# The second MLP matrix as seven half-block products for eight, aligned operand rings, and recurrent stages one behind the other

## The chip, the cores and the metric

The kernel runs on one core of a Trainium2 chip. Times are device microseconds of that core. Times that differ by less than about 0.2% cannot be told apart for this kernel (its three runs span 0.05%).

## The reference

The kernel computes two post-norm layers on a sequence of 1024 tokens of width 1024, in float32. Layer 0 mixes with sliding-window attention beside a gated DeltaNet, layer 1 with a Griffin recurrent block; each is followed by an MLP of hidden width 4096 with squared ReLU. What the change touches is this:

```
def rg_lru(x, w_a, b_a, w_x, b_x, lam):
    r = sigmoid(einsum('bthi,hij->bthj', xh, w_a) + b_a)
    i = sigmoid(einsum('bthi,hij->bthj', xh, w_x) + b_x)
    a = exp(-LRU_C * r * softplus(-lam))
    b = sqrt(-expm1(2 * log a)) * (i * x)
    h_t = a_t * h_{t-1} + b_t            (associative scan over time)

def recurrent_mixer(x, ...):
    xr, gate = split_cols(x @ w_in, (LRU_WIDTH, LRU_WIDTH))
    xr = causal_dwconv(xr, conv_w, conv_b)
    return (rg_lru(xr, ...) * gelu(gate)) @ w_out

def sqrelu_mlp(x, w1, w2):
    h = relu(x @ w1)
    return (h * h) @ w2

each layer:  x <- LN(alpha*x + mixer(x));  x <- LN(alpha*x + sqrelu_mlp(x))
```

## The kernel before

The 1024 tokens are worked as two chunks of 512, called stream 0 and stream 1. Each stream is a Python generator that runs hybrid mixer, output projection, layer norm, MLP of layer 0, layer norm, recurrent mixer (four `rec_block`s), output projection, layer norm, MLP of layer 1, layer norm. The only carry between streams is small (convolution halos, last recurrent state, attention keys).

**Precision.** Every large product is made of three float32r products: a value is split into a rounded high part and a low part, and `mm3` issues high x high, high x low and low x high into one PSUM bank. The split is a copy (mostly ScalarE, every fifth on VectorE) and a subtraction (alternately VectorE and GpSimd; `HV`, `LG`). Weights are split as they arrive (`wblock`: a 512 KB load into a `ws` tile, then tiles `wh` and `wl`); activations are split once.

**MLP.** `mlp` works through eight blocks `e` of 512 hidden units. For each of four slices `f` of 128 hidden units, `proj_fm` makes 24 matmuls of 128x512 (w1 stationary, all 512 tokens moving), then relu, square and split give two `s` tiles. Then w2 is applied: for each half of the output (512 columns), four PSUM banks (one for each 128 tokens) collect 4 slices x 3 matmuls with the `s` tile stationary and the weight moving, and VectorE adds each bank to the running output `y`, which lies in `g` tiles. That is 96 + 96 matmuls in a block and 8 additions from PSUM. The last block of the whole program has its weights split ahead and finishes token tile by token tile.

**Recurrent block.** One `rec_block` makes four projections of 24 matmuls (two with convolution, two for the gelu gate) and 24 gate matmuls, 120 in all, with tanh, exp, sqrt, a scan and products on ScalarE, VectorE and GpSimd in between.

**Order of the work.** All matmuls are put in one order by `Clock`, a rough model of the engines that asks at each step which generator's next product has its operands; small mixers (attention, DeltaNet, layer norm) come in between when their operands are due. The streams are taken by `phase` (0 goes first, and MLP 0 is phase 1, MLP 1 phase 2), so a recurrent block goes ahead of an MLP of the other stream and MLP matmuls fill its waits. Before the change, stream 0 waits behind its layer-0 MLP until stream 1 has its first layer norm (`ln1`), so the recurrent blocks of stream 0 lie beside stream 1's MLP of layer 0; stream 1 waits for `rec`, so its recurrent blocks lie beside stream 0's MLP of layer 1. The other engines take their work in the order in which it was written down; SyncE's queue issues the weight loads, ScalarE's a few others.

**Buffers.** `g`: 14 tiles of 2048 floats a partition; `t`, `s`, `f`: rings of 11, 9 and 4 tiles of 516 floats. A tile of 516 floats takes 2080 bytes, so every second tile of these rings starts 32 bytes off a multiple of 64; the tiles `g`, `ws`, `wh` and `wl` all start at multiples of 64.

## Time and profile before

| what | value |
|---|---|
| median of 3 runs | 2387.83 us (2387.71 to 2388.8) |
| span of the profiled execution | 2384.5 us, so 3.3 us of the median lie around it |
| granted TensorE clock, mean | 0.992 |
| TensorE busy | 2298.9 us (96%) |
| VectorE, ScalarE, GpSimd busy | 56%, 38%, 35% |
| DMA | 227.43 MB, mean 95 GB/s |

PE is TensorE's matmuls, PEld its weight loads (they overlap), DVE is VectorE, ACT ScalarE, POOL GpSimd. Nearly every instruction stands under one line, that of the helper which records it (L177 for the three elementwise engines, L204 for matmuls), so groups are read by tile names, `out<-in`. A matmul's row lasts about 0.39 us because matmuls are pipelined; what a matmul costs is the distance from one start to the next.

### The profile page before, as it was taken

The numbers are of one execution on the slowest core, as the hardware profiler recorded it, in microseconds if no ns is written. First come the engines' busy times: TensorE is split into PE (matmuls) and PEld (weight loads), VectorE is DVE, ScalarE is ACT, GpSimd is POOL, SyncE is SP. The second block draws the span as 40 slices with busy tenths as digits, with TensorE's granted clock in tenths as the row PEclk, the third lists the DMA queues.
The fourth block names the chain that finished last, engine by engine and source line by source line (L and its number), as shares of the span: only waits on it lengthen the run. The fifth ranks groups of instructions, "written<-read, shape, count | busy, mean of one in ns | idle before, by whom it ended". The sixth has DMA issues, their size and how long they took to land. (4 is left out here: it accounts for less than half of the span.)

```text
span 2384.5 us, 33354 instructions
## 1 busy us (share of the span) xinstructions
PE 2298.9 (96%) x12724; PEld 1841.9 (77%) x12724; DVE 1345.1 (56%) x2550; ACT 912.7 (38%) x1813; POOL 843.0 (35%) x706
## 2 busy tenths in 40 slices
PE   8889997999999999999999999999999999999997
PEld 7666775677777878778887788877887788778876
DVE  7697659565754463755664623565665543633345
ACT  5364424443333242454443322344554232322331
POOL 3342334232332243433443432343333333433341
PEclk9999998999999999999999999999999999999999
DMA  4121231122233222322333222232325222332231
GB/s 154 54 81 31 81 124 36 54 69 74 73 114 110 95 88 98 123 89 97 98 131 125 82 96 97 97 121 91 98 93 177 85 97 97 107 115 98 98 117 51
DMA packets 67487, 227.43 MB, mean 95 GB/s; under 512 B 7424, under 2 KB 7808, under 8 KB 67328
## 3 DMA queue, kind: packets, MB, share of 16 engines
q1 hardware_dynamic: 58832, 204.01, 25.9%
q10 hardware_dynamic: 8496, 21.30, 2.5%
q8 instruction: 100, 1.64, 0.3%
q14 instruction: 59, 0.48, 0.1%
HBM read 216.89 MB, written 8.39 MB: 94 GB/s over the span
## 5 line engine op out<-in xcount | busy, mean ns | idle before, releaser
L177 POOL TENSOR_TENSOR wl<-ws,wh 128x512 fp32r<-128x512 f32 (+1 forms) x372 | 497.6, 1338 | 1261.4 <-ACT wh L177 979.4
L204 PE MATMUL mm<-g,wh 128*128 128x512 f32 x2816 | 886.7, 396 | 0.5 <-DVE g L177 0.5
L177 ACT CAST wh<-ws 128x512 fp32r<-128x512 f32 (+1 forms) x595 | 365.5, 616 | 993.0 <-PE mm L204 910.1
L204 PE MATMUL mm<-wh,s 128*128 128x512 f32 x1984 | 648.2, 399 | 11.4 <-ACT s L177 5.7
L204 PEld LDWEIGHTS mm<-g,wh 128*128 128x128 f32 x2816 | 520.2, 189 | 107.2 <-issue 2.9
L204 PE MATMUL mm<-g,wl 128*128 128x512 f32 x1408 | 550.9, 391 | 5.4 <-POOL wl L177 5.4
L204 PEld LDWEIGHTS mm<-wh,s 128*128 128x128 f32 x1984 | 374.0, 189 | 102.6 <-ACT s L177 6.2
L204 PE MATMUL mm<-wl,s 128*128 128x512 f32 x992 | 391.9, 395 | 2.3 <-POOL wl L177 1.4
L177 DVE TENSOR_TENSOR wl<-ws,wh 128x512 fp32r<-128x512 f32 (+1 forms) x372 | 281.2, 756 | 188.8 <-ACT wh L177 184.4
L204 PEld LDWEIGHTS mm<-g,wl 128*128 128x128 f32 x1408 | 265.1, 188 | 64.0 <-POOL wl L177 7.1
L204 PE MATMUL mm<-wh,g 128*128 128x512 f32 (+1 forms) x768 | 235.2, 380 | 10.0 <-ACT wh L177 6.1
L177 DVE TENSOR_TENSOR s<-s,s 128x512 fp32r<-128x512 f32 x128 | 100.4, 784 | 242.9 <-POOL s L177 231.1
L204 PEld LDWEIGHTS mm<-wl,s 128*128 128x128 f32 x992 | 187.4, 189 | 43.3 <-POOL wl L177 1.8
L177 DVE TENSOR_TENSOR g<-g,mm 128x512 f32<-128x512 f32 x224 | 144.0, 680 | 130.7 <-PE mm L204 130.5
L204 PEld LDWEIGHTS mm<-wh,g 128*128 128x128 f32 x768 | 142.0, 190 | 38.7 <-ACT wh L177 6.1
L177 DVE CAST wh<-ws 128x512 fp32r<-128x512 f32 (+1 forms) x149 | 73.8, 495 | 172.6 <-PE mm L204 165.0
L177 POOL TENSOR_TENSOR s<-s 128x512 f32<-128x512 f32 x128 | 145.3, 1135 | 26.4 <-ACT s L177 26.4
L204 PE MATMUL mm<-wl,g 128*128 128x512 f32 (+1 forms) x384 | 143.7, 374 | 0.1
L177 ACT ACTIVATE s<-mm 128x512 f32<-128x512 f32 x128 | 75.9, 593 | 62.1 <-PE mm L204 61.9
L177 ACT ACTIVATE s<-s 128x512 fp32r<-128x512 f32 (+1 forms) x136 | 83.5, 614 | 19.0 <-DVE s L177 8.0
L204 PEld LDWEIGHTS mm<-wl,g 128*128 128x128 f32 x384 | 72.9, 190 | 11.9 <-DVE wl L177 0.4
L204 PE MATMUL mx<-g,wh 128*128 128x512 f32 x256 | 78.8, 389 | 0.0
(209 smaller groups left out, 2230.3 us busy)
## 6 DMA issues: line engine op xcount, KB each, us to landing
ws<-w SPq DMA_DIRECT2D x256, 512.0 KB, 3.3
ws<-hin_fm SPq DMA_DIRECT2D x32, 512.0 KB, 3.3
ws<-rin SPq DMA_DIRECT2D x32, 512.0 KB, 3.3
ws<-hout SPq DMA_DIRECT2D x16, 512.0 KB, 3.4
ws<-rout SPq DMA_DIRECT2D x16, 512.0 KB, 3.4
t<-ln ACTq DMA_DIRECT2D x28, 256.0 KB, 4.2
ws<-hin_q SPq DMA_DIRECT2D x8, 512.0 KB, 3.2
g<-x ACTq DMA_DIRECT2D x8, 512.0 KB, 5.0
```

The source lines that it names most:

```text
L177: r = f(*a, **k)
L204: return self._pe(self.pe.matmul(out, lhsT, rhs, start=start, stop=stop), out, [lhsT, rhs], c, start)
```

## The change

It has five parts.

1. **Seven products for eight** (`fast_w2`, `Fast`). A block's hidden activations (512 tokens x 512 hidden units) are seen as 2 x 2 blocks: two halves of 256 tokens, and the two slices of a pair `p`; w2 as two slices by two halves of the output. A Strassen form (with the sums of Winograd's variant) needs seven block products. Sums of activations (`s1` to `s4`) are formed in `hidden`, sums of weights (`t1` to `t4`) in `fast_w2`, in float32 before they are split. Four of the products are accumulated one on another in the same two PSUM banks (`X`), with the banks read between products; two others share a pair of banks (`R`). Every product's two banks are added to or subtracted from a quarter of `y`: 84 matmuls and 14 additions from PSUM. A block is worked so only where five `g` tiles are free when it begins (`begin`); the rest keep eight products. In the built program 23 of the 32 blocks are of the new kind, and the program has 10854 matmuls for 11130.
2. **The order within the MLP.** The first slice of block e+1 goes ahead of block e's w2 products.
3. **Rings and tiles.** `t` and `s` tiles are 512 floats, `f` tiles 528, so all start at multiples of 64 bytes; the `s` ring has 14 tiles. The DMA scratch area at the start of the memory is 1024 bytes for 16384. `wh` and `wl` are two tiles of 1024 floats for four of 512, so one copy and one subtraction split a whole load.
4. **w2 in another layout**: one load of 1 MB for a pair of slices, into a `g` tile (new blocks), or two strided 512 KB loads (old ones).
5. **Recurrent stages in a row.** Stream 0 waits until stream 1's layer-0 MLP has emitted its last w1 slice (`m7`), then the four blocks of both streams follow each other in turn (`rb`), stream 1's with `s` tiles for `t` tiles. The layer norm behind stream 1's output projection waits for `m7` of stream 0 (`hold`).

```diff
-WB, HV, LG = 4, 5, 2
-RINGS = dict(t=11, s=9, f=4)
+WB, WS, HV, LG = 2, 3, 5, 2
+RINGS = dict(t=11, s=14, f=4)
+FW = 528
...
     def tl(r, dt=F32):
-        return take(r, tpool.tile([P, 516], dt, tag=r, name=nm(r), bufs=RINGS[r]))
+        return take(r, tpool.tile([P, FW if r == "f" else 512], dt, tag=r, name=nm(r), bufs=RINGS[r]))
...
+    def split(h, l, x, key):
+        wcount[0] += 1
+        (V.tensor_copy if wcount[0] % HV == 0 else S.copy)(h, x)
+        (G if key else V).tensor_tensor(l, x, h, ALU.subtract)
...
+    def fast_w2(e, src, fast, hid, yg, ls):
...
+        for p in range(2):
+            DS.dma_start(fast.w[p], src[e * 2 + p])
+        X = [mm_ps() for _ in range(2)]
+        R = None
+        for i, (a, b, acc, out, sign, done) in enumerate((
+                ("a11", "b11", "X", (0, 0), 1, False), ("a12", "b21", "R", (0, 0), 1, True),
+                ("s2", "t2", "X", (0, 1), -1, False), ("s1", "t1", "R", (1, 1), 1, False),
+                ("s3", "t3", "X", (1, 1), -1, True), ("s4", "b22", "R", (0, 1), 1, True),
+                ("a22", "t4", "X", (1, 0), 1, True))):
+            if i in (1, 3):
+                R = [mm_ps() for _ in range(2)]
+            start = i in (0, 1, 3)
...
+                h, l = ts("t", F32R), ts("t", F32R)
+                split(h, l, x, (i + p) % 2)
+                if b == "b11":
+                    V.tensor_tensor(t1, b11, b12, ALU.add)
+                    V.tensor_tensor(t2, t1, b22, ALU.add)
+                    G.tensor_tensor(t3, b12, b22, ALU.add)
+                elif b == "b21":
+                    V.tensor_tensor(t4, t2, b21, ALU.add)
...
+            for p in range(2):
+                ah, al = hid[p][a]
+                for t in range(2):
+                    ps = (X if acc == "X" else R)[t]
+                    mm3(ps, ah[:, t * P:(t + 1) * P], al[:, t * P:(t + 1) * P], *hl[p], start and p == 0, p == 1, not start)
+                    if p == 1:
...
+                            V.tensor_tensor(y, y, ps, op)
...
+            S.activation(z, ps, AF.Relu)
+            S.activation(z, z, AF.Square)
+            if f % 2:
+                V.tensor_tensor(B[:, 0:512], A[:, 256:768], A[:, 512:1024], ALU.subtract)
+                V.tensor_tensor(B[:, 512:768], B[:, 256:512], A[:, 256:512], ALU.subtract)
+                V.tensor_tensor(B[:, 768:1024], A[:, 0:256], B[:, 512:768], ALU.add)
+                own = [ts("s", F32R) for _ in range(7)]
+                hl = [own[0:2], own[2:4], own[4:6], (own[6][:, 0:256], own[6][:, 256:512])]
+                for i, z in enumerate((A[:, 0:512], B[:, 512:1024], B[:, 0:512], A[:, 768:1024])):
+                    S.copy(hl[i][0], z)
+                    (G if i > 1 else V).tensor_tensor(hl[i][1], z, hl[i][0], ALU.subtract)
...
-        if c == 0:
-            yield from wait(lambda: "ln1" in st[1])
-        else:
-            yield from wait(lambda: "rec" in st[0])
         hT = ActT()
         light[c] = True
         for b in range(4):
+            yield from wait(lambda: c == 0 or sts[0].get("rb", 0) > b)
             if b % 2 == 0:
                 yield from need("g", 2)
-            yield from rec_block(c, b, s["x"], hT, s)
+            yield from rec_block(c, b, s["x"], hT, s, "ts"[c])
+            st[c]["rb"] = b + 1
```

**How the instructions move.** On TensorE, in the MLP of layer 1, before (`mm_` a PSUM bank, `wh`, `wl` the split weights that move, `s_` the stationary activations): the third slice of a half goes to four banks, which stay the block's banks over all four slices.

```order
L204 MATMUL mm_12845<-wh_12885,s_12796 128x512
L204 MATMUL mm_12845<-wl_12886,s_12796 128x512
L204 MATMUL mm_12845<-wh_12885,s_12797 128x512
L204 MATMUL mm_12846<-wh_12885,s_12796 128x512
L204 MATMUL mm_12846<-wl_12886,s_12796 128x512
L204 MATMUL mm_12846<-wh_12885,s_12797 128x512
L204 MATMUL mm_12847<-wh_12885,s_12796 128x512
L204 MATMUL mm_12847<-wl_12886,s_12796 128x512
```

After, in a block of the new kind (`t_` holds the split weight sums): the end of product `s4 x b22` in the `R` banks, and the start of `a22 x t4` in the `X` banks, which then hold their fourth product.

```order
L205 MATMUL mm_17694<-t_17744,s_17568 128x512
L205 MATMUL mm_17694<-t_17745,s_17568 128x512
L205 MATMUL mm_17694<-t_17744,s_17569 128x512
L205 MATMUL mm_17695<-t_17744,s_17568 128x512
L205 MATMUL mm_17695<-t_17745,s_17568 128x512
L205 MATMUL mm_17695<-t_17744,s_17569 128x512
L205 MATMUL mm_17616<-t_17762,s_17488 128x512
L205 MATMUL mm_17616<-t_17763,s_17488 128x512
L205 MATMUL mm_17616<-t_17762,s_17488 128x512
L205 MATMUL mm_17617<-t_17762,s_17488 128x512
```

Two token tiles share a product where there were four, and a bank is read and gone on with, not given back.

On VectorE, in the w2 part of a block in the MLP of layer 1, before: additions of banks to `y` (`g<-g,mm`) in fours, with weight splits between.

```order
L177 TENSOR_TENSOR g_16126<-g_16126,mm_19271 128x512
L177 TENSOR_TENSOR wl_19388<-ws_19385,wh_19387 128x512
L177 TENSOR_TENSOR g_16126<-g_16126,mm_19272 128x512
L177 TENSOR_TENSOR g_16127<-g_16127,mm_19273 128x512
L177 TENSOR_TENSOR g_16127<-g_16127,mm_19274 128x512
L177 CAST wh_19389<-ws_19385 128x512
L177 TENSOR_TENSOR wl_19426<-ws_19423,wh_19425 128x512
L177 TENSOR_TENSOR g_16126<-g_16126,mm_19347 128x512
```

After:

```order
L178 TENSOR_TENSOR g_14144<-g_14144,mm_17616 128x512
L178 TENSOR_TENSOR g_14144<-g_14144,mm_17617 128x512
L178 TENSOR_TENSOR s_17569<-g_17276,s_17568 128x512
L178 TENSOR_TENSOR t_17701<-g_17273,t_17700 128x512
L178 TENSOR_TENSOR g_14144<-g_14144,mm_17646 128x512
L178 TENSOR_TENSOR t_17719<-g_17272,t_17718 128x512
L178 TENSOR_TENSOR g_14144<-g_14144,mm_17647 128x512
L178 CAST t_17722<-g_17273 128x512
L178 TENSOR_TENSOR g_14144<-g_14144,mm_17616 128x512
L178 TENSOR_TENSOR g_14144<-g_14144,mm_17617 128x512
L178 TENSOR_TENSOR t_17745<-g_17273,t_17744 128x512
L178 TENSOR_TENSOR g_14145<-g_14145,mm_17694 128x512
```

Additions now come two for every product of 12 matmuls, with the splits of the next products queued between them, and bank 17616 is read four times in a block.

On ScalarE, in the recurrent stage, before (`f<-mm` the projection's copy, `s<-mm` the relu of the other stream's MLP):

```order
L177 ACTIVATE s_15021<-mm_14994 128x512
L177 ACTIVATE s_15019<-s_15021 128x512
L177 CAST g_14447<-t_14748 128x512
L177 CAST wh_15124<-ws_15122 128x512
L177 CAST g_14447<-t_14830 128x512
L177 COPY f_15026<-mm_15041 128x512
L177 ACTIVATE t_15028<-f_15026,sm 128x512
L177 ACTIVATE f_15027<-f_15026,sm 128x512
```

After:

```order
L178 COPY f_12540<-mm_12551 128x512
L178 CAST t_12452<-t_12451 128x512
L178 CAST g_12440<-s_12273 128x512
L178 ACTIVATE f_12541<-f_12540,sm 128x512
L178 ACTIVATE t_12542<-f_12540,sm 128x512
L178 CAST s_12498<-s_12497 128x512
L178 CAST wh_12670<-ws_12668 128x1024
L178 COPY f_12586<-mm_12597 128x512
```

No MLP work stands between any more: stream 0's block (`t` tiles) alternates with stream 1's (`s` tiles). From the first to the last matmul of the recurrent blocks the new order has 1264 matmuls: the blocks' own 960, 192 of stream 0's output projection, 64 transposes of layer norms and 48 of an MLP. Before, that stretch had 3568, of which 2352 were MLP.

## The prediction

> **What bounds the kernel now.** I read the page first, then the chain of waits, then stretches of time, then the groups of instructions by form, and last single rows. From the page, the span, the busy times, and TensorE's busy tenths in 40 slices:

> ```profile
> span 2384.5 us, 33354 instructions
> PE 2298.9 (96%) x12724; PEld 1841.9 (77%) x12724; DVE 1345.1 (56%) x2550; ACT 912.7 (38%) x1813; POOL 843.0 (35%) x706
> PE   8889997999999999999999999999999999999997
> ```

> TensorE works nearly throughout; only the first eight slices (the hybrid mixers) and the last show gaps. The chain of waits in order of time (start, length, engine and line, links) has long stretches of nothing else:

> ```profile
> 2089.11 223.08 PE mm L204 x971
> ```

> 223.08 us over 971 matmuls is 230 ns each: there matmul follows matmul, and taking matmuls out shortens the chain. Four stretches (busy us and counts of PE, PEld, DVE, ACT, POOL, then granted clock, DMA share, GB/s): MLP alone; the recurrent blocks of stream 0 beside stream 1's MLP; the stretch with the worst gap; the first fifth.

> ```profile
> 2100.00:2280.00 180.00, 180.00 (x786) 147.30 (x785) 56.83 (x94) 51.35 (x85) 58.68 (x49) 1.00 0.29 94
> 1000.00:1260.00 260.00, 257.90 (x1127) 211.01 (x1126) 146.30 (x188) 126.11 (x204) 96.48 (x89) 1.00 0.31 104
> 360.00:420.00 60.00, 44.91 (x394) 33.24 (x394) 55.85 (x135) 29.85 (x72) 28.05 (x21) 0.86 0.10 33
> 0.00:480.00 480.00, 433.53 (x3625) 329.13 (x3626) 353.79 (x892) 210.34 (x575) 170.09 (x160) 0.98 0.23 76
> ```

> In the MLP TensorE never stops and VectorE is busy 32% of the time. Where VectorE is at 74% (0 to 480) TensorE loses 10%, where it is at 93% (360 to 420) TensorE loses 25%. That is the measure for what follows: the change takes work from TensorE and gives work to VectorE and GpSimd.

> **Fewer matmuls.** The w2 matmuls by form (w2 is `wh,s` and `wl,s`):

> ```profile
> L204 PE MATMUL mm<-wh,s 128*128 128x512 f32 x1984 | 648.2, 399 | 11.4 <-ACT s L177 5.7 <-ACT f L177 4.2 <-DVE g L177 1.4
> L204 PE MATMUL mm<-wl,s 128*128 128x512 f32 x992 | 391.9, 395 | 2.3 <-POOL wl L177 1.4 <-DVE wl L177 0.9
> ```

> 1984 + 992 = 31 blocks of 96, with hardly a wait. The means near 400 ns are latencies; the price is the distance of starts. From the timeline, every third matmul of a w1 slice (`g,wl`) and of w2 (`wl,s`):

> ```profile
> 1940.05 0.39 PE L204 MATMUL mm<-g,wl 128*128 128x512 f32 x1
> ...
> 1947.53 0.39 PE L204 MATMUL mm<-g,wl 128*128 128x512 f32 x1
> ...
> 1948.67 0.39 PE L204 MATMUL mm<-wl,s 128*128 128x512 f32 x1
> ...
> 1969.56 0.40 PE L204 MATMUL mm<-wl,s 128*128 128x512 f32 x1
> ```

> w1: 11 triples in 7.48 us, 226.7 ns a matmul. w2: 30 triples in 20.89 us, 232.1 ns. The change removes 12 matmuls in each of 23 blocks, 276 in all: 276 x 232.1 = **-64.1 us**.

> **Aligned operands.** The two kinds of matmul differ in where their operands lie: `g`, `wh`, `wl` start at multiples of 64 bytes, `s` tiles only every second time. 2796 w2 matmuls remain; at w1's pace they save 2796 x 5.4 = 15.1 us, and if the 5.4 ns have another cause, nothing. Every stationary or moving operand in the changed program's w2 has w1's alignment, so I take two thirds, **-10 us**.

> **Elementwise work of a new block.** Unstalled prices from the timeline and the groups:

> ```profile
> 1922.07 1.29 POOL L177 TENSOR_TENSOR wl<-ws,wh 128x512 fp32r<-128x512 f32 x1 [5.55 <-ACT wh L177]
> 1924.06 0.43 DVE L177 CAST wh<-ws 128x512 fp32r<-128x512 f32 x1 [4.19 <-PE mm L204]
> 1924.53 0.69 DVE L177 TENSOR_TENSOR wl<-ws,wh 128x512 fp32r<-128x512 f32 x1
> L177 DVE TENSOR_TENSOR g<-g,mm 128x512 f32<-128x512 f32 x224 | 144.0, 680 | 130.7 <-PE mm L204 130.5
> ```

> Before, a block gives VectorE 3 casts, 12 subtractions and 8 additions from PSUM: 3 x 0.43 + 12 x 0.69 + 8 x 0.68 = 15.0 us; the MLP stretch shows 56.83 / (786/192) = 13.9, since neighbours overlap a little (factor 0.925). A new block has, in units of 512: 4 w1 subtractions, 4 units of activation sums, 4 of their splits, 7 weight splits, 6 weight sums, so 25 x 0.69; 4.4 casts; 14 additions from PSUM. That is 17.3 + 1.9 + 9.5 = 28.7, times 0.925 = 26.5 us. GpSimd has 4 + 3 + 7 + 2 = 16 units in 15 instructions, 16 x 1.29 = 20.6 us against 58.68 / 4.09 = 14.3. TensorE needs 180 x 0.228 = 41.0 us. VectorE goes from 32% to 65% before any waiting. And the two engines get in each other's way (start, duration, in the recurrent stage):

> ```profile
> 1208.37 1.47 POOL L177 TENSOR_TENSOR t<-t,f 128x512 f32<-128x512 f32 x1
> 1208.79 1.59 DVE L177 TENSOR_TENSOR wl<-ws,wh 128x512 fp32r<-128x512 f32 x1
> 1209.79 1.74 POOL L177 TENSOR_TENSOR wl<-ws,wh 128x512 fp32r<-128x512 f32 x1
> 1210.31 1.77 DVE L177 SCALAR_TENSOR_TENSOR t<-f,sm,t 128x512 f32<-128x512 f32 x1
> ```

> GpSimd's first ends at 1209.84, VectorE's 0.54 after it, GpSimd's next 1.15 after that, VectorE's next 0.55 after that: they take turns, and one held up costs VectorE 0.90 to 1.08 more. Taking turns, a new block needs 25 x 0.55 + 16 x 1.15 = 32.2 of 41.0 us (79%) for instructions that exclude each other; before, 12 x 0.55 + 8 x 1.15 + 4 x 0.9 = 19.4 of 44. If half of GpSimd's 15 instructions hold VectorE up by 1.0, it is at 34 of 41 us, 83%. TensorE has more lead here than in the stretch at 74% that lost 10% (splits run two products ahead in 11 `t` tiles), so I take 0.5 us a block: 23 x 0.5 = **+12 us**. Bounds: 0; and every one of the 15 holding it up by 1.08: 26.5 + 16.2 = 42.7, 1.7 over, +39 us.

> **Recurrent stages in a row.** Where they lie, by the halo copies and the last-state copies:

> ```profile
> L177 POOL COPY rhalo<-f x8: 191/652/661, 1010.5 to 1216.8; 128x3 f32<-128x3 f32 x8
> L177 POOL COPY rlast<-t x8: 298/655/709, 1067.4 to 1270.1; 128x1 f32<-128x1 f32 x8
> ```

> Stream 0's four blocks (4 x 120 = 480 matmuls) fill 1000 to 1260 with 647 of MLP. At the MLP's VectorE rate, 56.83/786 = 0.0723 us a matmul, the MLP has 46.8 of the 146.3 us, and the recurrent work 99.5/480 = 0.207 us a matmul against TensorE's 0.228: 91%. ScalarE by the same sum: (126.11 - 42.3)/480 = 0.175, 77%, and four more table loads. Until now the MLP's matmuls, at 32%, thinned this; that cover goes. 960 matmuls are 218 us: at the 25% lost at 93% it is more than 45 us, with two independent blocks alternating and nothing like the layer norm and the attention of that stretch, perhaps a third: 7%, **+15 us** (0 to 45).

> **Layer norms over new blocks.** A stretch of MLP with a layer norm and the next without:

> ```profile
> 1320.00:1380.00 60.00, 56.87 (x257) 46.05 (x256) 35.86 (x57) 25.78 (x43) 27.41 (x20) 0.97 0.24 79
> 1380.00:1440.00 60.00, 60.00 (x262) 48.98 (x261) 20.10 (x33) 15.33 (x26) 18.29 (x16) 1.00 0.30 97
> ```

> A layer norm brings VectorE 16 us. Over new blocks, at 34/41 x 60 = 50 us in 60, less than 10 are free: some 3 us more each, at three places, **+10 us** (0 to 20).

> **The rest.** The first output projection of stream 0 is now mixed with stream 1's DeltaNet work instead of lying before it, so the 15 us gap at 360 to 420 should shrink: -5 (-12 to +5). The new blocks' 1 MB loads replace two of 512 KB; DMA is at a 0.30 share. They wait in SyncE's queue until the block before has split its last weights, with the w1 loads queued behind; cover is the hidden projections (21 us). Splitting a load in one piece makes TensorE's first use wait for 1024 elements; a slice of 24 matmuls (5.4 us) covers a copy and GpSimd's some 2.5 us. I cost both at nothing; uncovered they would be part of the +39.

> **Sum.** -64.1 - 10 + 12 + 15 + 10 - 5 = -42.1. The profiled span is 2384.5, and 3.3 us lie around it in the median: 2384.5 - 42.1 + 3.3 = **2346 us**.

> **Rivals.**
> *All cover holds.* Full alignment gain, no stall: -64.1 - 15.1 - 5, 2304 us. For it: no MLP stretch of before lost anything, and every engine's sum stays under TensorE's. Against it: 83% and 91%.
> *The bank is read too late (slower).* An accumulator must be read before the product after next adds to it, so VectorE has one product, 12 x 0.227 = 2.72 us, for a subtraction queued ahead and two reads: 0.69 + 0.68 + 0.68 fits, with the subtraction held up by 1.08 it is 3.13, 0.41 late. In all seven products of 23 blocks that is 66 us instead of 12: -42.1 + 54 gives 2400 us. It decides from 0.34 us a product on. [...]
> *The recurrent row starves TensorE.* 45 instead of 15: 2376 us. For it: 91% and one `f` ring of four for both streams.

> **Chances.** Forecast 0.55 (2325 to 2370), all cover 0.20, late banks 0.13, recurrent row 0.12. What cannot be told from no change is 0.2%, 4.8 us. All cover, nearly all of the forecast and most of the third rival are faster: 0.80; same 0.06; slower 0.14. The range runs from the first rival to just short of the second: 2303 to 2392.

> **What the changed profile would show.** 1932 matmuls `mm<-t,s`, triples every 0.680 us (right) or 0.696 (alignment does nothing). MLP stretches with TensorE at 98% or more, VectorE near 50 in 60, GpSimd near 30: right; TensorE under 94% there, waiting for `DVE g`: the second rival. The recurrent stretch, 1264 matmuls, some 300 us long with 15 us of gaps; 45 is the third. I am wrong if gaps stand anywhere else, above all in the first fifth, whose order moved too.

## The result, and the profile after

The changed kernel takes **2468.15 us** (median of 4 runs, 2466.11 to 2472.24) against 2388.32 us (2387.71 to 2389.1) before: a ratio of **1.0334, 95% interval 1.0319 to 1.0348**. It is slower by 80 us where 42 us less were forecast. The page of the changed kernel:

```profile
span 2467.1 us, 32823 instructions
PE 2279.1 (92%) x12448; PEld 1814.0 (74%) x12448; DVE 1790.9 (73%) x2862; ACT 1025.0 (42%) x1884; POOL 1045.1 (42%) x679
PE   8989998999999897999997799989999997989987
DVE  6788586647544589488889777685588889688885
PE 53%; DVE 28%; ACT 7%; issue 6%; POOL 3%; DMA 3%; ACTq 0%; DVEq 0%; SPq 0%; POOLq 0%
```

276 matmuls are gone and TensorE's busy time is 20 us less, but its idle time is 2467.1 - 2279.1 = 188 us, where it was 85.6. VectorE's 28% in the chain of waits (fourth part of the page, last row above), the largest share after TensorE's own, point to VectorE. What TensorE waited for, from the view of waits (total us, times, longest; `mx` are the mixers' PSUM banks, and `mx L209` are transposes, most of them behind layer norms), and then the groups by form (busy, mean ns, then idle time before them and what ended it):

```profile
PE mm L205 <- DVE s L178: 39.3, 13, 6.2
PE mm L205 <- POOL wl L178: 21.8, 13, 3.5
PE mm L205 <- ACT s L178: 16.9, 6, 6.7
PE mx L209 <- DVE g L178: 16.2, 5, 11.4
PE mm L205 <- DVE g L178: 8.5, 16, 2.5
```

```profile
L205 PE MATMUL mm<-t,s 128*128 128x512 f32 x1932 | 473.5, 403 | 65.6 <-DVE s L178 38.6 <-ACT s L178 16.9 <-DVE g L178 8.1
L178 ACT CAST t<-g 128x512 fp32r<-128x512 f32 x256 | 154.2, 619 | 400.4 <-DMA g<-w 145.0 <-DVE g L178 129.7 <-PE mm L205 116.3
L178 DVE TENSOR_TENSOR g<-g 128x512 f32<-128x512 f32 x138 | 178.3, 1293 | 68.9 <-ACT g L178 58.6 <-POOL t L178 9.0
L178 DVE TENSOR_TENSOR t<-g,t 128x512 fp32r<-128x512 f32 x161 | 157.2, 978 | 17.2 <-ACT t L178 13.4 <-PE mm L205 2.0 <-POOL t L178 0.5
```

The new blocks' matmuls (`mm<-t,s`, 23 blocks of 84) stood still for 65.6 us, mostly for an `s` tile, the split hidden activations. I counted the waits by their place in the block, 12 matmuls a product: 55.2 of the 65.6 us stand in the **first** product, which takes 127.6/23 = 5.55 us where the last takes 62.6/23 = 2.72. The third row of the groups shows VectorE's sums at 1293 ns, where the same form takes 0.69 us with nothing beside it.

One such start, in time order (start, length, engine; some rows, most of them matmuls and weight loads, are left out):

```profile
2155.65 0.60 ACT L178 ACTIVATE g<-mm 128x512 f32<-128x512 f32 x1 [1.54 <-PE mm L205]
2156.66 0.63 ACT L178 ACTIVATE g<-g 128x512 f32<-128x512 f32 x1
2157.32 0.63 ACT L178 CAST s<-g 128x512 fp32r<-128x512 f32 x1
2159.19 1.76 DVE L178 TENSOR_TENSOR g<-g 128x512 f32<-128x512 f32 x1 [1.18 <-POOL t L178]
2160.36 2.84 POOL L178 TENSOR_TENSOR wl<-ws,wh 128x1024 fp32r<-128x1024 f32 x1
2160.87 2.88 DVE L178 TENSOR_TENSOR t<-g,t 128x512 fp32r<-128x512 f32 x1
2160.89 1.97 PE L205 MATMUL mm<-t,s 128*128 128x512 f32 x8
2163.16 1.71 POOL L178 TENSOR_TENSOR g<-g 128x512 f32<-128x512 f32 x1
2163.67 1.48 DVE L178 CAST t<-g 128x512 fp32r<-128x512 f32 x1
2165.07 1.28 DVE L178 TENSOR_TENSOR g<-g 128x512 f32<-128x512 f32 x2
2166.28 0.68 DVE L178 TENSOR_TENSOR g<-g,g 128x512 f32<-128x512 f32 x1
2166.88 0.68 DVE L178 TENSOR_TENSOR s<-g,s 128x512 fp32r<-128x512 f32 x1
2167.61 0.80 PE L205 MATMUL mm<-t,s 128*128 128x512 f32 x1 [4.74 <-DVE s L178]
```

Relu, square and cast of the last projection are done at 2157.95. The subtraction that TensorE needs (`s<-g,s`) runs at 2166.88, behind four sums, a split and a cast. Beside GpSimd's 2.84 us split of 1024 elements VectorE's split takes 2.88 us for 0.69 and ends 0.55 us after it; the cast, 0.41 us when alone, takes 1.48.

That stall cost more than its 4.74 us: behind it the granted clock was 0.50. Stretches right after the stall above in the changed kernel, and after a single stall of 2.86 us in the kernel before (busy us and counts of PE, PEld, DVE, ACT, POOL, then granted clock):

```profile
2167.60:2171.00 3.40, 3.39 (x8) 2.74 (x9) 3.40 (x3) 1.88 (x4) 2.38 (x2) 0.50 0.00 0
```

```profile
1900.80:1904.20 3.40, 3.11 (x7) 2.49 (x8) 3.40 (x4) 0.83 (x3) 2.77 (x3) 0.50 0.00 0
1904.20:1908.00 3.80, 3.80 (x20) 3.10 (x19) 3.80 (x4) 1.02 (x2) 3.80 (x3) 1.00 0.31 92
```

For 3.4 us the granted clock is 0.50 and 8 matmuls start where 15 would at 226.7 ns. The mean granted clock is 0.970 against 0.992 before, and the clock records of both traces hold 1.0 and 0.5 alone: at half speed for (1 - 0.970)/0.5 = 6% of 2467.1 us, 148 us, against 38 us. That is up to (148 - 38)/2 = 55 us of TensorE's time; as TensorE was busy in only 103 us of the one and 24 of the other, it is by estimate some (103 - 24)/2 = 40 us. My sum had no term for it.

### The profile page after: what moved, and what is told of

It is laid out like the page before. It is cut to its first block, busy times and chain, and to the rows that moved or that the text cites. A ratio compares the mean times of both kernels' runs of the same rounds, so it can differ in the third digit from the quotient of the medians.

```text
span 2467.1 us, 32823 instructions
## 1 busy us (share of the span) xinstructions
PE 2279.1 (92%) x12448; PEld 1814.0 (74%) x12448; DVE 1790.9 (73%) x2862; ACT 1025.0 (42%) x1884; POOL 1045.1 (42%) x679
## 4 chain that ended last, share of the span: by engine, by line
PE 53%; DVE 28%; ACT 7%; issue 6%; POOL 3%; DMA 3%; ACTq 0%; DVEq 0%; SPq 0%; POOLq 0%
PE mm L205 44%; DVE g L178 12%; PE mx L205 7%; DVE t L178 6%; DVE s L178 3%; DMA g<-w 2%; DVE hsc L178 2%; DVE wl L178 2%; DVE f L178 2%; ACT g L178 2%; POOL wl L178 2%; ACT wh L178 1%; ACT t L178 1%; PE mx L209 1%; ACT s L178 1%
## 5 line engine op out<-in xcount | busy, mean ns | idle before, releaser
L178 POOL TENSOR_TENSOR wl<-ws,wh 128x1024 fp32r<-128x1024 f32 (+1 forms) x140 | 350.9, 2506 | 602.5 <-ACT wh L178 452.5
L205 PE MATMUL mm<-t,s 128*128 128x512 f32 x1932 | 473.5, 403 | 65.6 <-DVE s L178 38.6
L205 PEld LDWEIGHTS mm<-t,s 128*128 128x128 f32 x1932 | 369.3, 194 | 161.6 <-DVE s L178 44.3
L178 ACT CAST wh<-ws 128x1024 fp32r<-128x1024 f32 (+1 forms) x226 | 234.1, 1036 | 398.9 <-PE mm L205 344.3
L178 ACT CAST t<-g 128x512 fp32r<-128x512 f32 x256 | 154.2, 619 | 400.4 <-DMA g<-w 145.0
L178 POOL TENSOR_TENSOR t<-g,t 128x512 fp32r<-128x512 f32 x161 | 240.9, 1505 | 130.1 <-PE mm L205 67.5
L178 DVE TENSOR_TENSOR g<-g,mm 128x512 f32<-128x512 f32 x362 | 240.7, 680 | 60.1 <-PE mm L205 59.3
L178 DVE TENSOR_TENSOR wl<-ws,wh 128x1024 fp32r<-128x1024 f32 (+1 forms) x140 | 184.0, 1314 | 109.4 <-ACT wh L178 107.2
L178 DVE TENSOR_TENSOR g<-g 128x512 f32<-128x512 f32 x138 | 178.3, 1293 | 68.9 <-ACT g L178 58.6
L178 POOL TENSOR_TENSOR s<-g,s 128x512 fp32r<-128x512 f32 x92 | 127.8, 1404 | 121.5 <-ACT s L178 116.8
L205 PE MATMUL mm<-wh,s 128*128 128x512 f32 x512 | 169.3, 399 | 2.8 <-DVE f L178 2.8
L178 DVE TENSOR_TENSOR t<-g,t 128x512 fp32r<-128x512 f32 x161 | 157.2, 978 | 17.2 <-ACT t L178 13.4
L178 ACT CAST s<-g 128x512 fp32r<-128x512 f32 (+1 forms) x184 | 101.1, 564 | 131.3 <-DVE g L178 130.1
L178 POOL TENSOR_TENSOR g<-g 128x512 f32<-128x512 f32 x46 | 70.8, 1540 | 130.3 <-DVE g L178 127.9
L205 PEld LDWEIGHTS mm<-wh,s 128*128 128x128 f32 x512 | 96.9, 189 | 24.2 <-DVE f L178 3.4
```

The lines of the kernel that those rows point to most:

```text
L178: r = f(*a, **k)
L205: ins = self.pe.matmul(out, lhsT, rhs, start=start, stop=stop, skip_group_check=fresh)
```

## The experiments

The theories that the expectations weigh: VectorE too full (A), the late single-buffered load of w2 (B), the wide splits (C), the recurrent row (D), too short a lead for the hidden activations (E), GpSimd holding VectorE up (F), the order of VectorE's queue (G). A ratio is that to the kernel before.

**The parts of the change, one by one.** The operands' place alone, on the kernel before:

```diff
+FW = 528
...
-        return take(r, tpool.tile([P, 516], dt, tag=r, name=nm(r), bufs=RINGS[r]))
+        return take(r, tpool.tile([P, FW if r == "f" else 512], dt, tag=r, name=nm(r), bufs=RINGS[r]))
...
-    nc = _bacc.Bacc("TRN2", target_bir_lowering=False, num_devices=1)
+    nc = _bacc.Bacc("TRN2", target_bir_lowering=False, num_devices=1, dynamic_dma_scratch_size=1024)
```

> The kernel before with one thing of the change: every tile of the rings t and s 512 elements wide (2048 bytes) instead of 516, the f tiles 528, so that all operands of the w2 matmuls start at multiples of 64 bytes. The order of instructions is that of the kernel before on every engine. In the changed kernel the remaining w2 matmuls start every 227 ns where they started every 232 before. If the operands' place is the cause, 3072 w2 matmuls save 5.4 ns each, 16 us, and other matmuls with an s or t tile may add some: 2388.3 - 16 = 2372 us, with mm<-wl,s triples every 0.680 us. If the pace came from the swapped roles of weights and activations (s tiles now stand still, the weights move) nothing changes here: 2388 us, triples every 0.696 us.

**2375.55 us, ratio 0.9948 (0.9933 to 0.9963)**: faster than both kernels, and the only part of the change that pays. Timeline of its w2 part, the second matmul (`wl`) of each triple:

```profile
1940.87 0.39 PE L205 MATMUL mm<-wl,s 128*128 128x512 f32 x1
...
1961.95 0.39 PE L205 MATMUL mm<-wl,s 128*128 128x512 f32 x1
```

31 triples in 21.08 us, 226.7 ns a matmul. Only places in memory differ from the kernel before, so the place of the operands is the cause.

Then the changed kernel without the new blocks:

```diff
-                if fast[0] is None and (c == 1 or sts[1].get("op", -1) >= layer) and rings["g"] >= 5:
+                if False and fast[0] is None and (c == 1 or sts[1].get("op", -1) >= layer) and rings["g"] >= 5:
```

> The changed kernel with every MLP block in the old form (eight half-block products): no sums, no shared banks, the alignment, the splits of 1024 elements, the first hidden projection ahead of the block before and the recurrent stages in a row all stay. If the loss lies in the new blocks alone, the recurrent row costs the 15 us that I predicted or less and this is 2388 - 16 + 15 = 2387 us or below. If the row itself loses the 46 us that the stage sum shows in the changed kernel, with 1024-wide splits behind it, it is 2388 - 16 + 46 = 2418 us. If the 1024-wide splits with two buffers starve the hidden projections everywhere (TensorE waited 21.8 us for POOL wl), the MLP stretches show TensorE under 98% here too and the time is above 2430 us.

2428.2 us, 1.0167 (1.0150 to 1.0184): half of the loss is there without a single new block. The same with the recurrent stages put back where they were:

```diff
+        if c == 0:
+            yield from wait(lambda: "ln1" in st[1])
+        else:
+            yield from wait(lambda: "rec" in st[0])
...
-            yield from wait(lambda: c == 0 or sts[0].get("rb", 0) > b)
...
-            yield from rec_block(c, b, s["x"], hT, s, "ts"[c])
+            yield from rec_block(c, b, s["x"], hT, s, "t")
```

> The changed kernel with all MLP blocks in the old form and the recurrent stages where they lay before the change, beside the other stream's MLP; wide splits, alignment and the hidden projection ahead stay. Theory D: the row's 55 us go, 2372 to 2385 us. Theory C: the wide splits starve the recurrent blocks here too, 2400 us or more.

2398.48 us, 1.0045 (1.0030 to 1.0060). So the ladder from the kernel before is: alignment -13, wide splits with the projection ahead and w2's layout +23, recurrent row +30, new blocks +40 (2468.2 - 2428.2). It is one order of the steps; another could share the total out differently. How the +23 divides was not measured, but with old stages TensorE waits 25.1 us for `wl` tiles here, against 7.9 in the run with the alignment alone, which points to the wide splits. Now the row, in the kernel without new blocks: most of its stretch, and the longest wait ahead of it (view of waits, 1350 to 1620):

```profile
1427.00:1660.00 233.00, 210.67 (x877) 167.59 (x876) 167.58 (x198) 143.39 (x202) 82.19 (x54) 0.95 0.34 113
```

```profile
PE mx L209 <- DVE g L178: 18.1, 1, 18.1
```

In the 233 us TensorE is idle for 22.3, and a mean clock of 0.95 is, by the same estimate, half clock for a tenth of them, up to some 12 us more; the recurrent stretch of the kernel before, 1000 to 1260, lost 2.1 of 260 us. VectorE is at 72% and ScalarE at 62%, so no engine is full. The single wait of 18.1 us ends at 1358.6: it is for the layer norm ahead of the row, beside which no MLP is left to work on. With the old stages all waits of this kind together are 1.1 us.

**Narrow splits**, in the changed kernel and in the one without new blocks:

```diff
-        split(h, l, st, wcount[0] % LG)
+        for i, (h, l) in enumerate(hl):
+            split(h, l, st[:, i * m:(i + 1) * m], (wcount[0] + 1) % LG == 0)
```

> The changed kernel with the w1 and mixer weights split in two pieces of 512 elements into four buffers, as before the change, instead of one of 1024 into two; the new blocks, their sums and the recurrent row stay. Theory C, the wide splits (GpSimd's wl takes 2.4 us at 1024 elements, holds a VectorE instruction beside it up for as long, 1996.15 2.78 for 0.69 us, and the first matmul on wl waits for the whole piece: 33 us of waits for POOL wl and DVE wl): a good part of those 33 us and of the late s tiles goes, with the clock that comes back slowly after each some 30 to 50 us: 2420 to 2440 us. If only the amount of VectorE's work counts (theory A), which is the same here but for 140 fixed costs of some 0.06 us: 2460 to 2475 us.

> The changed kernel with all MLP blocks in the old form (2428 us) and the narrow splits as well: what is left of the change is the alignment, the recurrent stages in a row and the hidden projection ahead. Theory C for the row: the 1024-wide splits make the recurrent blocks late (272 us of matmul distances against 218 in the kernel with the alignment alone), then 2385 to 2395 us here. Theory D, the row itself, VectorE and ScalarE at 47 and 43 of 60 us without an MLP between, and the layer norm ahead of it with nothing beside (one wait of 18.1 us): 2415 to 2428 us.

2443.41 us (1.0230, 1.0213 to 1.0248) and 2419.71 us (1.0137, 1.0121 to 1.0152): 25 and 8.5 us back. The first has 21 new blocks instead of 23, the order having moved, which is worth some 3 us of the 25 at 40/23 us a block. So wide splits hurt most beside the new blocks. Without new blocks undoing them gives back only 8.5 us, so most of the row's 30 us is not theirs.

**What in the new blocks costs.** Four edits of the changed kernel, one at a time (the main lines of each are shown): the weight sums over 8 columns; w2 loaded only for the first new block of an MLP; GpSimd's part over 8 columns; GpSimd's part given to VectorE. The first three leave work out.

```diff
+                t1, t2, t3, t4, b12, b21, b22, b11 = (z[:, :8] for z in (t1, t2, t3, t4, b12, b21, b22, b11))
...
-            DS.dma_start(fast.w[p], src[e * 2 + p])
+            if fast.loaded:
+                clk.issue("D", [fast.w[p]], [src[e * 2 + p]], fast.w[p].nbytes() / 360e3, 0.0, 2.0)
+            else:
+                DS.dma_start(fast.w[p], src[e * 2 + p])
...
+        if key == 8:
+            clk.n = 512
+            G.tensor_tensor(l[:, :8], x[:, :8], h[:, :8], ALU.subtract)
...
-                split(h, l, x, (i + p) % 2)
+                split(h, l, x, 0)
```

> The changed kernel with the four sums of weights of each half block taken over 8 of their 512 columns (and the product of t2 split from b12): what it leaves out is VectorE's 6 x 0.69 and GpSimd's 2 x 1.29 us in each of 23 blocks, so the output is not the reference's. TensorE's order is that of the changed kernel. Theory A, VectorE too full (50 of 60 us busy with hold-ups by GpSimd, the splits of the hidden activations late): 23 x 4.1 = 95 us less for VectorE, most of the 65 us of waits at the start of the new blocks and half of those of the hidden projections go: 2468 - 60 to 100 = 2370 to 2410 us. Theory B, ScalarE held in order behind the late 1 MB load (145 us of its idle time): the load still waits for the last split of the block before: 2445 to 2468 us.

> The changed kernel with w2's 1 MB loads only for the first new block of each MLP; later blocks split what the sums left there, so the output is not the reference's. TensorE's order is that of the changed kernel. Theory B, the single buffer of w2 (the load is issued when the block before has split its last weights; ScalarE stands in order behind it for 145 us in all, and the relu and the splits of the hidden activations behind ScalarE): the 145 us go, the s tiles come in time, and most of the 95 us lost in the new blocks is back: 2360 to 2400 us. Theory A, VectorE too full: the late load only fills time that ScalarE has over: 2445 to 2468 us.

> The changed kernel with GpSimd's part of the new blocks (half the splits of the weights, half the splits of the activations, one sum) over 8 columns instead of 512; the matmuls take the first part of a split number where that second part would have been read, so the output is not the reference's. VectorE's own instructions, their number and sizes stay, TensorE's number of matmuls too. VectorE's time over its unheld durations is 375 us in the changed kernel against 205 before. Theory F, hold-ups: they go in the new blocks (170 us), and as the sums' 95 us of VectorE's own gave 60 us, this gives as much or more: 2350 to 2410 us. Theory A in its narrow form, only the instructions of VectorE itself count and GpSimd's company is free: 2450 to 2468 us.

> The changed kernel with GpSimd's part of the new blocks given to VectorE: nothing is left out. VectorE gets 16 units of 0.69 us more per block (11.0 us, at its overlap of 0.925 some 10.2) and loses the hold-ups, 170/23 = 7.4 us per block. Theory F: the two nearly cancel and the chains get shorter by GpSimd's 1.29 against 0.69, 2440 to 2475 us. If the hold-ups cost less than they seem (the held instruction would have waited anyway), VectorE at 28.7 + 11 = 37 of 41 us a block is the bound: 2500 us or more.

| changed kernel, but | median us | ratio (95%) | `mm<-t,s` waits, us | first product, us a block |
|---|---|---|---|---|
| (as it is) | 2468.15 | 1.0334 (1.0319 to 1.0348) | 65.6 | 5.55 |
| sums over 8 columns | 2408.22 | 1.0083 (1.0068 to 1.0098) | 36.2 | 4.20 |
| one load of w2 | 2434.33 | 1.0195 (1.0180 to 1.0210) | 45.0 | 4.70 |
| GpSimd's part over 8 columns | 2382.44 | 0.9977 (0.9968 to 0.9986) | 17.3 | 3.58 |
| GpSimd's part on VectorE | 2447.02 | 1.0248 (1.0234 to 1.0262) | 57.9 | 5.19 |

The late load (theory B) is worth 34 us, the sums 60, GpSimd's company 86. They cannot simply be added, for that is more than the new blocks lose: a chain can be late for several reasons at once. In the run with GpSimd's part away, VectorE executes the same instructions as in the changed kernel (L179 here is L178 there):

```profile
PE 2252.7 (95%) x12448; PEld 1808.0 (76%) x12448; DVE 1636.2 (69%) x2862; ACT 1023.1 (43%) x1884; POOL 706.8 (30%) x679
L179 DVE TENSOR_TENSOR t<-g,t 128x512 fp32r<-128x512 f32 x161 | 118.7, 745 | 29.1 <-ACT t L179 25.3
```

Its busy time falls by 155 us and the mean of its split from 978 to 745 ns. Theory A in its narrow form falls; theory F stands, and here GpSimd's help costs more than it saves: with the same work all on VectorE the kernel is 21 us faster. How much of the 86 us is hold-up and how much GpSimd's own length in the chain was not separated.

**Moving the wait.** A longer lead for the hidden activations (a second projection ahead of the new block), then the same with narrow splits:

```diff
                     yield from hidden(e + 1, 0, nxt)
+                    if early:
+                        yield from hidden(e + 1, 1, nxt, True)
```

> The changed kernel with one thing moved: the second hidden projection of the next block (its 24 matmuls, relu and square, without its sums and splits) also goes ahead of the new block, so that between the last hidden projection of a block and its first product TensorE has two projections (10.9 us) of other work, not one (5.4 us). Nothing is added or left out. Theory E, the lead: 55 of the 66 us that TensorE waits in the new blocks stand at the first of the seven products (5.5 us in place of 2.7, all others at pace), because relu, square, three sums, copies and splits of the last projection go through a full VectorE in less than 6.8 us of cover. With 12.3 us of cover these 55 us go and half-speed clock with them: 23 x 2.8 = 65 us at most, 2400 to 2425 us. Theory A, only the amount of VectorE's work counts: the wait moves elsewhere, 2455 to 2475 us.

> The changed kernel with narrow splits (2443 us) and the longer lead. Theory E with theory C beside it, if both add up: 2443 - 45 to 60 = 2383 to 2398 us, what is left over the kernel before being the recurrent row (30 us) against the matmuls taken out (58 us) and the alignment (13 us) with the stalls that remain. If narrow splits had already given the lead back, under 15 us of gain: 2430 us or more.

2490.81 us (1.0429, 1.0411 to 1.0448) and 2441.0 us (1.0216, 1.0201 to 1.0231): theory E falls as a cure. The first product's wait does go, from 55.2 to 9.9 us, but the fourth's grows from 3.7 to 39.4, and the transposes behind the layer norms (first row) wait 52.3 us where they waited 16.2. From the changed kernel with the longer lead:

```profile
PE mx L209 <- DVE g L178: 52.3, 12, 11.4
PE mm L205 <- DVE g L178: 39.7, 36, 4.6
PE mm L205 <- DVE s L178: 8.7, 5, 2.6
```

`mm <- DVE g` are late reads of banks: there are four `mm` banks, the fourth product takes a new pair `R`, and it waits for the additions that read the second product's. That is the kind of wait of the prediction's second rival, small until the first wait was taken away. Then VectorE's queue in another order, weight sums behind the activation splits:

```diff
-                    V.tensor_tensor(t1, b11, b12, ALU.add)
+                    ins = V.tensor_tensor(t1, b11, b12, ALU.add)
+                    clk.tc.add_manual_dep(ins.ins, fast.split.ins.name, NOSYNC, reason="order")
```

> The changed kernel with one thing about the order of VectorE's queue: the sums of a new block's weights stand behind the splits of the last hidden activations, which that block's first product needs, instead of ahead of them. Work, loads, widths, splits and TensorE's order are those of the changed kernel. Theory G, the order of the queue: in the changed kernel the split of the activations was ready for VectorE at 2157.95 and ran at 2166.88, behind a split and four sums of weights, and TensorE stood still for 4.7 us; with the sums behind it, some 40 of the 55 us at the first product go with the clock that they cost: 2400 to 2430 us. Theory F alone, hold-ups and VectorE's fill: the sums are then late for the third product, as the longer lead moved the wait to the fourth: 2450 to 2475 us.

**2593.72 us, 1.0851 (1.0835 to 1.0868)**, 126 us worse than the changed kernel:

```profile
PE mm L205 <- DVE t L178: 73.0, 26, 6.4
PE mm L205 <- ACT t L178: 63.7, 18, 4.1
PE mm L205 <- DVE s L178: 15.7, 8, 2.9
```

The first product's wait fell to 24.7 us, the third's, the first to use a weight sum, rose from 1.6 to 148.7. Theory G falls as a cure: in both orders one of the two chains comes late, and in the order of the changed kernel it was the cheaper one.

**Is any form of the new blocks worth having?** Old stages, narrow splits, six new blocks in the MLP that runs alone; then with the lead; with w2 loaded a block ahead; with the old order of projections for old blocks; with GpSimd's part on VectorE; with the queue order:

> The changed kernel with the recurrent stages where they lay before and the narrow splits; there is room for new blocks only in six blocks of one MLP, which leaves 72 matmuls out, 16.3 us at 226.7 ns. If a new block costs more than it saves wherever it stands (40 us over 23 blocks in the changed kernel against its form without them, 1.7 us each): 2375 + 10 = 2385 us. If it pays where splits are narrow and no other stage runs beside it: 2375 - 16 to 2375 - 8, that is 2359 to 2367 us, faster than both kernels.

> The kernel with old stages, narrow splits and six new blocks (2384 us), with the same longer lead. In it the first of the seven products took 4.8 us in place of 2.7, the fourth 3.8 and the new blocks together 141.6 us against 504 x 0.2267 = 114. Theory E: the first product's 12.7 us and some more go, 2368 to 2374 us, which is at or under the kernel with the alignment alone (2375.5). Theory A: 2380 to 2385 us.

> The kernel of old stages, narrow splits, six new blocks and longer lead, with a second buffer for w2's 1 MB: a block's weights are loaded before the block ahead of it begins. Theory B for what is left: ScalarE no longer stands behind the load (6 us a block), 5 to 10 us less than the same kernel with one buffer, 2360 to 2367 us. If the lead already covers the load, the two are the same within 2 us.

```diff
-            self.w = self.g[:2]
+            self.ws = [self.g[:2], self.g[5:]]
...
+                if nxt["fast"] is not None:
+                    load(e + 1, nxt["fast"])
```

> Old stages, narrow splits, alignment, old order of hidden projections wherever the old form stands; six new blocks in the one MLP that runs alone, with the longer lead and w2 loaded a block ahead. The kernel with the alignment alone takes 2375.5; these six blocks took 21.1 us each in the run with early loads against 96 x 0.230 = 22.1: 2375.5 - 6 + 0 to 4, 2368 to 2374 us, if the place of the hidden projection was what cost the old blocks 17 us there.

> The same with GpSimd's part of the six new blocks on VectorE. With nothing else beside these blocks VectorE is at 26.5 + 10.2 = 36.7 of 41 us without hold-ups, against 34 with them. Theory F: equal or up to 5 us less than its pair (the chain to the first product gets shorter). If the amount on VectorE decides: 5 to 12 us more.

> The kernel with old stages, narrow splits, six new blocks with lead, early loads and their GpSimd part on VectorE (2377.3 us), and the same order of VectorE's queue. Its six new blocks lose 9 us against pace (123.3 against 114.3). Theory G: 3 to 6 us of these go, 2371 to 2375 us. Theory F alone: within 2 us of 2377.

| six new blocks | median us | ratio (95%) | new blocks' w2, us a block |
|---|---|---|---|
| single load | 2384.1 | 0.9985 (0.9976 to 0.9994) | 23.6 |
| + lead | 2382.91 | 0.9974 (0.9963 to 0.9985) | 23.1 |
| + early load | 2378.32 | 0.9957 (0.9942 to 0.9972) | 20.7 |
| + old order of projections | 2378.65 | 0.9962 (0.9950 to 0.9975) | 20.8 |
| + GpSimd's part on VectorE | 2377.32 | 0.9958 (0.9944 to 0.9971) | 20.6 |
| + queue order | 2392.63 | 1.0017 (1.0008 to 1.0026) | 23.3 |

(The times from one start to the next of a block's 84 matmuls, each wait counted to the matmul that waited; pace is 19.0, an old block's 96 take 21.8 at that pace.) With the load early and this MLP running alone, a new block does save a microsecond. Yet none of the six beats the alignment alone (2375.55): the medians of the best three lie 2 to 3 us above it, and the intervals overlap. What takes the six microseconds back is open; it is not the projection ahead, for the old order changes nothing (2378.65 for 2378.32). The early load pays most here (theory B, 4.6 us). The queue order costs 15 us here too, with 8.6 us of waits at the third product, where there was none.

**What was expected and missed.** Nine of the eighteen times lie outside every range that was given. Five lie between two theories or close beside one: the changed kernel without new blocks, the same with old stages, narrow splits, one load of w2, and the early load (4.6 us, where 5 to 10 or under 2 were expected). The longer lead, both queue orders and the old order of projections came out slower than any of their theories allowed.

## Why the prediction was wrong, point by point

- **Fewer matmuls, -64.1**: the 276 are gone. Right.
- **Aligned operands, -10 (0 to -15.1)**: right; -13 when measured alone, the remaining w2 at 226 to 227 ns.
- **Elementwise work of a new block, +12 (0 to +39), with layer norms +10 (0 to 20)**: this failed. The new blocks cost +40 where -64.1 + 22 was forecast, so the two terms measured 40 + 62.6 = 103 us (276 matmuls at 226.7 ns are 62.6), 4.5 us a block in place of about 1, above both upper ends together. The 103 also hold what late loads and wide splits cost beside the new blocks (next item). The load was right: VectorE at about 50 of 60 us, GpSimd 33 to 37 (I had near 30), hold-ups of the size quoted (the sums `g<-g` that began under a GpSimd instruction took 1.77 us, those with none beside them 0.69). What it does to TensorE was mis-sized (stretches of the changed kernel):

```profile
1960.00:2020.00 60.00, 56.87 (x246) 45.51 (x245) 49.99 (x59) 26.73 (x46) 36.03 (x23) 1.00 0.28 96
2020.00:2080.00 60.00, 46.91 (x197) 37.57 (x196) 54.32 (x67) 21.17 (x36) 32.59 (x21) 0.86 0.22 79
2160.00:2220.00 60.00, 52.70 (x215) 40.96 (x214) 51.42 (x58) 24.96 (x42) 33.17 (x22) 0.94 0.26 88
2260.00:2320.00 60.00, 59.79 (x264) 48.94 (x263) 51.70 (x67) 24.59 (x44) 36.53 (x23) 1.00 0.32 114
```

  I had set up the measure myself (74% of VectorE loses 10% of TensorE's time, 93% loses 25%), and for 83% took 1.2%, arguing that TensorE has more lead there. By that measure it is near 17%, 7 us a block; measured were 4.5 of 41, 11%. But the share is no price either: in the last two rows VectorE is equally busy, and TensorE loses 7.3 us in one stretch and 0.2 in the other. What counts is whether a chain is in time. The lead I named, splits two products ahead, is that of the weights; the activations had one projection, 5.4 us, for a chain that took 11.9 in the timeline above. The upper bound, work over capacity, was no bound: a chain can be late on an engine that is not full. The second row shows a layer norm over such blocks, 13 us lost in 60 where 3 were expected.
- **Loads and wide splits at nothing**: failed. The load was not covered by the 21 us of projections: ScalarE waited 145.0 us for `g<-w`, and with one load only it is 34 us less. Undoing the wide splits gives back 8.5 us without new blocks and some 22 with them. I had set 5.4 us of cover against GpSimd's 2.5 for TensorE's first use; that VectorE's split takes 2.88 us beside GpSimd's of 2.84, for 0.69 (timeline above), was not in that sum.
- **Recurrent row, +15 (0 to 45)**: +30, inside its bounds, but made up otherwise. Gaps were foreseen (22 us for 15), from a VectorE at 91% of TensorE's time; it is at 72%. The lower clock there, 0.95 on average, and the wait of 18.1 us for the layer norm ahead of the row were not foreseen.
- **First output projection, -5 (-12 to +5)**: inside its bounds.

```profile
0.00:480.00 480.00, 442.11 (x3664) 334.17 (x3665) 347.34 (x890) 214.40 (x574) 166.39 (x136) 0.98 0.23 75
```

  In the changed kernel TensorE is busy for 8.6 us more in the first 480 than the 433.53 of before.
- **The clock**: no term at all; some 40 us by estimate, at most 55, spread over the terms above.
- **Rivals**: "all cover holds" fell. "The bank is read too late" was not what happened: 8.5 us of waits for `DVE g` in the changed kernel; waits for banks do appear with the longer lead. "The row starves TensorE" was two thirds right in size, and not the main loss. None of them put the wait at the first product. My own sign of being wrong, gaps anywhere else, came true there and at the layer norms, not in the first fifth.

## What to carry to other kernels

Trading matmuls for elementwise work paid here, by a microsecond a block, only where the elementwise chains had time, and lost 40 us over 23 blocks where they had not: list for each product the chain that feeds it, with hold-ups, against the TensorE work between. The busy share of the engine does not price it: here the same share cost TensorE between 0.2 and 7.3 us in 60. Look at the granted clock behind a stall too: here, behind one of 4.74 us, it was 0.50 for 3.4 us. Before moving a stage, see which waits its neighbours were covering. A wait at one place may cover a wait at the next; before moving it, see what else is due at the same time.

## What the runs showed that I had not expected

- With all operands at multiples of 64 bytes, a 128x512 matmul whose stationary operand is a 128x128 part of a split tile took 226.7 ns where it took 232.1 before; nothing but the places of tiles was changed in that run.
- In the changed kernel, up to the last matmul, half-clock stretches last 3.41, 6.83 or 10.24 us, whole steps of one grid, and all but one follow a step with 1.89 us or more of idle time. There 9 of 13 stalls between 2 and 3 us lie in such a stretch or within 1 us of one, and 2 of 50 between 0.3 and 1 us.
- Casts on VectorE, which have one input, took longer beside GpSimd too. In the changed kernel 31 casts `t<-g` that began under a GpSimd instruction took 1.23 us on average, three that began in the last 0.05 us of one 0.41, the 32 with none beside them 0.42. Additions from a PSUM bank did not take longer: their mean is 680 ns, as before the change, and the 145 that began under a GpSimd instruction took 0.68 us.

```profile
L178 DVE TENSOR_TENSOR g<-g,mm 128x512 f32<-128x512 f32 x362 | 240.7, 680 | 60.1 <-PE mm L205 59.3
```
